# Four groups instead of six through DRAM, fetched one pair earlier, in a mixture of experts

## The chip, the cores and the metric

The kernel runs on one core of one Trainium2 chip. The metric is the device time of one execution in microseconds; the time before is the median of three runs.

## The reference, cut

The program is two blocks of two layers each on 256 tokens of width 1024, in float32. Each layer ends with a hierarchical mixture of experts. What is computed in the first block, where the change is:

```python
def hier_moe(h, wgc, bgc, wgf, bgf, w1, w3, w2):       # 16 experts of width 256, two for each token
    ...                                               # gates: [T, 16], two entries of a row are not zero
    a = jnp.einsum('td,edf->tef', t, w1)
    c = jnp.einsum('td,edf->tef', t, w3)
    act = jax.nn.silu(a) * c * gates[:, :, None].astype(t.dtype)
    y = jnp.einsum('tef,efd->td', act, w2)
    return y.reshape(B, S, D)

# in first_block, for each of its two layers
y_moe = hier_moe(h, ...)
y_ple = jax.nn.sigmoid(h @ ple_wg[i] + ple_bg[i]) * (p[i] @ ple_wp[i])
h = layer_norm(DN_ALPHA * h + y_moe + y_ple, ln2_g[i], ln2_b[i])
```

## The kernel before

The program is written with the Tile framework: the source gives the order of the work, and a scheduler that works at compile time puts every engine's instructions into one fixed queue, in which they run in order; it may move an instruction ahead of earlier ones that it thinks will still wait. `self.behind(r)` (L581) makes what is traced in it stand behind instruction `r` on `r`'s engine.

Weights come from DRAM in tiles of 1 MB, issued by SyncE in the order in which they are used (`w_ahead`, L555). They share 22 slots of 8 KB per partition (`s8`, `NS`) with most of the other large tiles; a new tile waits until the last reader of what was in its slot is done. PSUM's eight banks are two sets of four, `pp` (products that are held) and `ps` (called `pa` in the trace).

`experts` (L1316) is used by both blocks; `far` is true in the first one alone. There each expert has 64 places for tokens, two experts make a group of 128 rows, eight groups are worked on in four pairs (`j` = 0, 2, 4, 6). For a pair:

- `gather` (L1328) brings the tokens of a pair's experts into columns by products with a matrix of zeros and ones (`rD`), one pair ahead.
- `up` (L1346) multiplies by w1 and w3 (32 matmul instructions per group: `pa<-w,xg`). Between the two halves of a pair's second `up` stands `turn` of its first group.
- `turn` (L1358) makes the gated product: SiLU on ScalarE (L1361), a multiplication on VectorE (L1362), two transposes on TensorE (L617), a copy on ScalarE (L1367).
- `down(j, q)` (L1372) multiplies by half `q` of w2 (8 instructions). For the first six groups (`out`) the result goes to a `pp` bank, is copied to SBUF, by ScalarE or VectorE (L1391, L1389), and is written to a table `rows` in DRAM by GpSimd's DMA queue (L1392). For the last two it goes to a `ps` bank and is split into a high and a low part (`split`, L613, L614).
- `fetch` (L1398), at the end of the third pair, brings for each token its at most two rows of the table back by four indirect DMAs on GpSimd's queue (L1403) into two slots `yz`, and adds them to `h` with eight additions on VectorE (L1408). A token without a second row there reads row 0, which is zero. `row_ids` (L1245) works out which rows.
- `combine` (L1413) takes the last two groups back to the tokens by products with the transposed matrix (`rS`, made by `spread`, L1262, with four transposes for a pair of groups, L1271), which add up in four `pp` banks `y`: per group 2 parts x 2 halves x 2 token tiles. `residual` (L644) adds `h` into `y` by products with the identity. The layer norm reads `y`.

The hook `each(j)` runs other work between these steps: in layer 0 the steps of the next layer's filters (on `ps` banks), in layer 1 a piece of the second block's preparation.

In the trace layer 0's mixture lies from about 185 to 315 us, layer 1's from about 500 to 625 us; the last pairs begin at 273.49 and 577.84 us.

Of the kernel before, what the change touches and what calls it, by code (L numbers as in the profile page):

```python
# [12 lines left out]
F32 = mybir.dt.float32  # L13
# [8 lines left out]
D = 1024  # L22
# [8 lines left out]
E1, CAP1 = 16, 64  # L31
E2, CAP2 = 32, 32
NS = 22

AHEAD = {"10": (6, 8, 11, 13, 10), "11": (6, 8, 11, 13, 10), "20": (6, 10, 12, 16, 16), "21": (6, 10, 12, 16, 16)}
WPRI = 20
# [433 lines left out]
class Kern:  # L470
# [303 lines left out]
    def setup(self):  # L774
        nc, I = self.nc, self.I
        self.h = self.s8([128, 2, D], "h")
        self.pc = self.const([128, I["pc"].shape[1]], name="pc")
        for t in range(2):
            nc.sync.dma_start(self.h[:, t, :], I["x"][t * 128:(t + 1) * 128, :])
        nc.sync.dma_start(self.pc, I["pc"])  # L780
        self.ident = self.const([128, 128], name="ident")
        make_identity(nc, self.ident)

        def cut(name, **k):
            o, n = self.L["pc"][name]
            a = self.pc[:, o:o + n]
            return a.rearrange("p (a b) -> p a b", **k) if k else a

        self.rc = cut("rc", a=2)
        self.rs = cut("rs", a=2)  # L790
        self.iota = cut("iota")
        self.key = cut("key")
        self.inv2 = cut("inv2")
        self.identb = self.const([128, 128], BF16, name="identb")
        nc.gpsimd.tensor_copy(self.identb, self.ident)
        self.oneb = self.const([128, 128], BF16, name="oneb")
        nc.gpsimd.memset(self.oneb, 1.0)
        self.ones = self.const([128, 1], name="ones")
        nc.gpsimd.memset(self.ones, 1.0)
        self.identr = self.const([128, 128], F32R, name="identr")  # L800
        nc.gpsimd.tensor_copy(self.identr, self.ident)
        self.selm = self.const([128, 36], name="selm")
        nc.gpsimd.tensor_add(self.selm, self.ident[:, 0:36], self.ident[:, 64:100])

        self.rows = self.dpool.tile([1 + (E1 - 4) * CAP1, D], F32, name="rows")
        zero = self.tmp(D // 128)
        nc.gpsimd.memset(zero, 0.0)
        nc.gpsimd.dma_start(self.rows[0:1, :].rearrange("a (p c) -> (a p) c", p=128), zero)
        self.emask = {}
        for cap in sorted({CAP1, CAP2}):  # L810
            ne = 128 // cap
            m = self.const([128, 2, ne], name=f"em{cap}")
            nc.gpsimd.memset(m, 0.0)
            for i in range(ne):
                nc.gpsimd.memset(m[i * cap:(i + 1) * cap, :, i], 1.0)
            self.emask[cap] = m
# [428 lines left out]
    def row_ids(self, r):  # L1245

        v, cap, E = self.nc.vector, r["cap"], r["E"]
        z = self.tmp(5 * E + 4)
        s, u, base = a2(z[:, 0:2 * E]), a2(z[:, 2 * E:4 * E]), z[:, 4 * E:5 * E]
        v.tensor_scalar(base, self.iota[:, 0:E], float(cap), -float(cap), op0=OP.mult, op1=OP.add)  # L1250
        v.scalar_tensor_tensor(s, r["pos"], float(cap), r["pos"], op0=OP.is_le, op1=OP.mult)
        v.scalar_tensor_tensor(u, s, 0.0, base[:, None, :].to_broadcast([128, 2, E]), op0=OP.is_gt, op1=OP.mult)
        v.tensor_add(s, s, u)
        near = 2 * (128 // cap)
        f = a2(z[:, 5 * E:])
        v.reduce_max(f[:, 0], s[:, :, 0:E - near], axis=AX)
        v.reduce_sum(f[:, 1], s[:, :, 0:E - near], axis=AX)
        v.tensor_sub(f[:, 1], f[:, 1], f[:, 0])
        r["ids"] = a2(r["free"].bitcast(I32))
        v.tensor_copy(r["ids"], f)  # L1260
# [55 lines left out]
    def experts(self, r, th, tl, pre, affine, y=None, each=None, later=(0, 1), begun={}):  # L1316
# [4 lines left out]
        cap, ns = r["cap"], r["ns"]  # L1321
        ne = 128 // cap
        ng = ns // 128
        xgs, pgs, aTs = {}, {}, {}
        gain, shift = affine
        far = y is None

        def gather(b):  # L1328
            if b != 1:
# [28 lines left out]
        def turn(j):  # L1358
            pg = pgs.pop(j)
            a = self.tmp(256)  # L1360
            nc.scalar.activation(a, pg[:, 0:256], AF.Silu, scale=1.0 if r["row"] is None else r["factor"][:, j:j + 1])  # L1361
            v.scalar_tensor_tensor(a, a, r["gate"][:, j:j + 1], pg[:, 256:512], op0=OP.mult, op1=OP.mult)  # L1362
            pt = self.ps()
            for f in range(2):
                self.transp(pt[:, f * 128:(f + 1) * 128], a[:, f * 128:(f + 1) * 128])
            aT = a2(self.tmp(256))
            nc.scalar.activation(aT, a2(pt[:, :256]), AF.Copy)  # L1367
            aTs[j] = aT
# [3 lines left out]
        def down(j, q):  # L1372

            aT = aTs[j]
            c = width(j)
            out = far and j < ng - 2
            py = self.pp() if out else self.ps()
            n, o = q * c // 512, q * c % 512
            for f in range(2):
# [18 lines left out]
        def fetch():  # L1398

            z = [self.s8([128, 2, D], "yz") for _ in range(2)]  # L1400
            for t in range(2):
                for k in range(2):
                    nc.gpsimd.indirect_dma_start(z[k][:, t, :], None, self.rows, bass.IndirectOffsetOnAxis(ap=r["ids"][:, k, t:t + 1], axis=0))  # L1403
            for t in range(2):
                for n in range(2):
                    x = self.h[:, t, n * 512:(n + 1) * 512]
                    for k in range(2):
                        v.tensor_add(x, x, z[k][:, t, n * 512:(n + 1) * 512])  # L1408

        def width(j):  # L1410
            return D // ne if j == ng - 1 else 512

        def combine(j, qs, start=False):  # L1413

            if j not in r["S"]:
                self.spread(r, [j, j + 1])
            c = width(j)
            for z in range(2):
                for q in qs:
# [21 lines left out]
        for j in range(0, ng, 2):  # L1441
# [8 lines left out]
            down(j, 1)  # L1450
            if each:
                each(j + 1)
            if last:
                if far:
                    y = [[self.pp(), self.pp()] for _ in range(2)]
                    combine(j, (0, 1), True)
                    down(j + 1, 0)
                    self.residual(v, y)
                    self.h = self.s8([128, 2, D], "h")
                    down(j + 1, 1)  # L1460
                    combine(j + 1, (0, 1))
                    continue
                self.h = self.s8([128, 2, D], "h")
                combine(j, (0, 1))
                for q in range(D // width(j + 1)):
                    down(j + 1, q)
                    if q:
                        combine(j + 1, (q - 1,))
                combine(j + 1, (q,))
            elif far:  # L1470
                for q in range(2):
                    down(j + 1, q)
                gather(j // 2 + 1)
                if j + 4 == ng:
                    fetch()
                    self.spread(r, [ng - 2, ng - 1])
            else:
                down(j + 1, 0)
                combine(j, (0, 1))
                down(j + 1, 1)  # L1480
                gather(j // 2 + 1)
                combine(j + 1, (0, 1))
# [674 lines left out]
```

## Time and profile before

| | before |
|---|---|
| median of 3 runs | 1358.36 us (1356.62 to 1360.59) |
| profiled execution | 1358.84 us, span 1357.2 us, mean granted TensorE clock 0.951 |
| TensorE busy (matmul) | 1215.0 us, 90% |
| VectorE, ScalarE, GpSimd busy | 647.1, 471.1, 69.6 us |
| read from and written to HBM | 399.94 MB, 7.34 MB |
| GpSimd's DMA queue | 10.49 MB in 3104 packets |

Busy time is a sum over stages with different limits, and a matmul's end is modelled, so 90% doesn't say that TensorE is at its peak. What a stage is worth is read from the timeline of its engines and from what ended each wait. A time in the rows below is in microseconds from the start of the span. PE is TensorE's matmul, PEld its weight load, DVE VectorE, ACT ScalarE, POOL GpSimd, SP SyncE; `x16` counts instructions that the timeline has merged, and an fp32 product counts as two.

### The profile page before, as it was taken

The numbers are of one execution on the slowest core, as the hardware profiler recorded it, in microseconds if no ns is written. First come the engines' busy times: TensorE is split into PE (matmuls) and PEld (weight loads), VectorE is DVE, ScalarE is ACT, GpSimd is POOL, SyncE is SP. The second block draws the span as 40 slices with busy tenths as digits, with TensorE's granted clock in tenths as the row PEclk, the third lists the DMA queues.
The fourth block names the chain that finished last, engine by engine and source line by source line (L and its number), as shares of the span: only waits on it lengthen the run. The fifth ranks groups of instructions, "written<-read, shape, count | busy, mean of one in ns | idle before, by whom it ended". The sixth has DMA issues, their size and how long they took to land. (4 is left out here: it accounts for less than half of the span.)

```text
span 1357.2 us, 17894 instructions
## 1 busy us (share of the span) xinstructions
PE 1215.0 (90%) x6512; PEld 735.0 (54%) x6512; DVE 647.1 (48%) x1840; ACT 471.1 (35%) x971; POOL 69.6 (5%) x95
## 2 busy tenths in 40 slices
PE   6999999979999999958999888787899998978877
PEld 5777754427877763415888432231498676413222
DVE  6867853338778961227776410110487556101011
ACT  4456521215565631205665210110356652100011
POOL 1200000010200000110011000000000101000000
PEclk8899999989999999979999898898999998989989
DMA  9455579996254669998074899999950537999997
GB/s 379 176 206 217 192 276 403 422 414 265 78 218 166 246 238 409 422 414 352 26 280 159 315 413 421 421 422 421 394 238 33 224 118 295 422 421 422 421 421 260
DMA packets 71537, 408.55 MB, mean 301 GB/s; under 512 B 7952, under 2 KB 18448, under 8 KB 26128
## 3 DMA queue, kind: packets, MB, share of 16 engines
q1 hardware_dynamic: 68336, 396.82, 73.0%
q0 software_dynamic: 3104, 10.49, 1.9%
q8 instruction: 54, 0.88, 0.3%
q14 instruction: 43, 0.35, 0.1%
HBM read 399.94 MB, written 7.34 MB: 300 GB/s over the span
## 5 line engine op out<-in xcount | busy, mean ns | idle before, releaser
L604 PE MATMUL pa<-w,xg 128*32 128x512 f32 (+1 forms) x1536 | 304.4, 673 | 52.4 <-DMA w<-in_w 49.5
L604 PEld LDWEIGHTS pa<-w,xg 128*32 128x32 f32 (+1 forms) x1536 | 79.6, 131 | 251.3 <-issue 148.3
L596 DVE TENSOR_TENSOR wlo<-w,whi 128x512 fp32r<-128x512 f32 (+1 forms) x260 | 177.3, 692 | 47.2 <-PE pp L604 37.4
L594 ACT ACTIVATE whi<-w 128x512 fp32r<-128x512 f32 (+1 forms) x260 | 157.9, 628 | 115.8 <-PE pp L604 99.5
L1362 DVE SCALAR_TENSOR_TENSOR tmp<-tmp,rgs,pa 128x256 f32<-128x256 f32 x32 | 15.4, 480 | 308.0 <-ACT tmp L1361 307.8
L604 PE MATMUL pa<-w,tmp 128*32 128x512 f32 (+2 forms) x640 | 122.1, 556 | 10.4 <-DMA w<-in_w 10.2
L614 DVE TENSOR_TENSOR wlo<-pa,whi 128x512 fp32r<-128x512 f32 (+1 forms) x44 | 28.3, 643 | 140.9 <-ACT whi L613 138.5
L604 PE MATMUL pp<-wlo,hTh 128*128 128x512 f32 (+1 forms) x224 | 87.7, 395 | 1.8 <-DVE wlo L596 1.8
L604 PE MATMUL pp<-whi,hTh 128*128 128x512 f32 (+1 forms) x224 | 88.7, 396 | 0.0
L604 PE MATMUL pp<-whi,hTl 128*128 128x512 f32 (+1 forms) x224 | 87.8, 392 | 0.0
L604 PE MATMUL pp<-hTh,wlo 128*128 128x256 f32 x256 | 73.8, 289 | 3.8 <-DVE wlo L596 3.8
L604 PE MATMUL pp<-hTh,whi 128*128 128x256 f32 x256 | 74.3, 291 | 2.5 <-DVE hTh L901 2.5
L604 PE MATMUL pp<-hTl,whi 128*128 128x256 f32 x256 | 73.3, 287 | 0.0
L604 PE MATMUL pa<-rD,th 128*128 128x256 f32 x256 | 67.7, 301 | 1.3 <-DVE row L699 0.8
L604 PEld LDWEIGHTS pa<-w,tmp 128*32 128x32 f32 (+1 forms) x640 | 29.4, 112 | 71.2 <-issue 43.2
L1361 ACT ACTIVATE tmp<-pa,rgs 128x256 f32<-128x256 f32 x16 | 7.6, 473 | 171.5 <-PE pa L604 171.5
L613 ACT ACTIVATE whi<-pa 128x512 fp32r<-128x512 f32 (+1 forms) x44 | 24.6, 558 | 121.2 <-PE pa L604 121.2
L604 PE MATMUL pa<-rD,tl 128*128 128x256 f32 x256 | 65.3, 292 | 0.0
L604 PEld LDWEIGHTS pa<-rD,th 128*128 128x128 f32 x256 | 51.0, 199 | 16.2 <-issue 12.4
L1367 ACT ACTIVATE tmp<-pa 128x256 f32<-128x256 f32 x32 | 12.2, 382 | 127.0 <-PE pa L617 127.0
L604 PEld LDWEIGHTS pp<-hTh,whi 128*128 128x128 f32 x256 | 50.1, 196 | 5.1 <-ACT whi L594 3.4
L604 PEld LDWEIGHTS pp<-hTh,wlo 128*128 128x128 f32 x256 | 50.2, 196 | 4.6 <-DVE wlo L596 4.6
(473 smaller groups left out, 2080.7 us busy)
## 6 DMA issues: line engine op xcount, KB each, us to landing
w<-in_w SPq DMA_DIRECT2D x349, 1024.0 KB, 16.4
w<-in_w SPq DMA_DIRECT2D x32, 256.0 KB, 6.0
gb<-in_row SPq DMA_DIRECT2D x5, 1024.0 KB, 14.2
w<-in_w SPq DMA_DIRECT2D x8, 512.0 KB, 20.5
rows<-whi POOLq DMA_DIRECT2D x12, 256.0 KB, 6.7
rows<-wlo POOLq DMA_DIRECT2D x12, 256.0 KB, 7.1
FI<-in_c SPq DMA_DIRECT2D x4, 512.0 KB, 7.7
w<-in_w SPq DMA_DIRECT2D x2, 640.0 KB
```

The source lines that it names most:

```text
L594: self.nc.scalar.activation(hi, w[:, c0:c0 + c], AF.Copy)
L596: self.nc.vector.tensor_sub(lo, w[:, c0:c0 + c], hi.bitcast(F32))
L604: self.last = self.nc.tensor.matmul(out, lhsT, rhs, start=start, stop=True, skip_group_check=True)
L613: self.nc.scalar.activation(hi, x, AF.Copy)
L614: self.nc.vector.tensor_sub(lo, x, hi.bitcast(F32))
L1361: nc.scalar.activation(a, pg[:, 0:256], AF.Silu, scale=1.0 if r["row"] is None else r["factor"][:, j:j + 1])
L1362: v.scalar_tensor_tensor(a, a, r["gate"][:, j:j + 1], pg[:, 256:512], op0=OP.mult, op1=OP.mult)
L1367: nc.scalar.activation(aT, a2(pt[:, :256]), AF.Copy)
```

## The change

Only groups 0 to 3 go through the DRAM table (`NFAR = 4`). The fetch stands at the end of the second pair, with the spread of groups 4 to 7 behind it. The additions are a function of their own, called in the third pair, and are held behind the VectorE multiplication of group 5's gated product (`turned[nf + 1]`). Groups 4 and 5 are split and combined as the last two are; the four banks `y` are taken in the third pair, and the combine of group 4 starts the sums. The residual's products stand ahead of the last pair's combine. The second block takes the same path as before.

```diff
@@ -31,6 +31,7 @@
 E1, CAP1 = 16, 64
 E2, CAP2 = 32, 32
 NS = 22
+NFAR = 4
 
 AHEAD = {"10": (6, 8, 11, 13, 10), "11": (6, 8, 11, 13, 10), "20": (6, 10, 12, 16, 16), "21": (6, 10, 12, 16, 16)}
 WPRI = 20
@@ -802,7 +803,7 @@
         self.selm = self.const([128, 36], name="selm")
         nc.gpsimd.tensor_add(self.selm, self.ident[:, 0:36], self.ident[:, 64:100])
 
-        self.rows = self.dpool.tile([1 + (E1 - 4) * CAP1, D], F32, name="rows")
+        self.rows = self.dpool.tile([1 + NFAR * 128, D], F32, name="rows")
         zero = self.tmp(D // 128)
         nc.gpsimd.memset(zero, 0.0)
         nc.gpsimd.dma_start(self.rows[0:1, :].rearrange("a (p c) -> (a p) c", p=128), zero)
@@ -1251,10 +1252,10 @@
         v.scalar_tensor_tensor(s, r["pos"], float(cap), r["pos"], op0=OP.is_le, op1=OP.mult)
         v.scalar_tensor_tensor(u, s, 0.0, base[:, None, :].to_broadcast([128, 2, E]), op0=OP.is_gt, op1=OP.mult)
         v.tensor_add(s, s, u)
-        near = 2 * (128 // cap)
+        fe = NFAR * 128 // cap
         f = a2(z[:, 5 * E:])
-        v.reduce_max(f[:, 0], s[:, :, 0:E - near], axis=AX)
-        v.reduce_sum(f[:, 1], s[:, :, 0:E - near], axis=AX)
+        v.reduce_max(f[:, 0], s[:, :, 0:fe], axis=AX)
+        v.reduce_sum(f[:, 1], s[:, :, 0:fe], axis=AX)
         v.tensor_sub(f[:, 1], f[:, 1], f[:, 0])
         r["ids"] = a2(r["free"].bitcast(I32))
         v.tensor_copy(r["ids"], f)
@@ -1321,9 +1322,10 @@
         cap, ns = r["cap"], r["ns"]
         ne = 128 // cap
         ng = ns // 128
-        xgs, pgs, aTs = {}, {}, {}
+        xgs, pgs, aTs, turned = {}, {}, {}, {}
         gain, shift = affine
         far = y is None
+        nf = NFAR if far else 0
 
         def gather(b):
             if b != 1:
@@ -1359,7 +1361,7 @@
             pg = pgs.pop(j)
             a = self.tmp(256)
             nc.scalar.activation(a, pg[:, 0:256], AF.Silu, scale=1.0 if r["row"] is None else r["factor"][:, j:j + 1])
-            v.scalar_tensor_tensor(a, a, r["gate"][:, j:j + 1], pg[:, 256:512], op0=OP.mult, op1=OP.mult)
+            turned[j] = v.scalar_tensor_tensor(a, a, r["gate"][:, j:j + 1], pg[:, 256:512], op0=OP.mult, op1=OP.mult)
             pt = self.ps()
             for f in range(2):
                 self.transp(pt[:, f * 128:(f + 1) * 128], a[:, f * 128:(f + 1) * 128])
@@ -1373,7 +1375,7 @@
 
             aT = aTs[j]
             c = width(j)
-            out = far and j < ng - 2
+            out = j < nf
             py = self.pp() if out else self.ps()
             n, o = q * c // 512, q * c % 512
             for f in range(2):
@@ -1401,19 +1403,22 @@
             for t in range(2):
                 for k in range(2):
                     nc.gpsimd.indirect_dma_start(z[k][:, t, :], None, self.rows, bass.IndirectOffsetOnAxis(ap=r["ids"][:, k, t:t + 1], axis=0))
+            return z
+
+        def add(z):
+
             for t in range(2):
                 for n in range(2):
                     x = self.h[:, t, n * 512:(n + 1) * 512]
                     for k in range(2):
-                        v.tensor_add(x, x, z[k][:, t, n * 512:(n + 1) * 512])
+                        with self.behind(turned[nf + 1]):
+                            v.tensor_add(x, x, z[k][:, t, n * 512:(n + 1) * 512])
 
         def width(j):
             return D // ne if j == ng - 1 else 512
 
         def combine(j, qs, start=False):
 
-            if j not in r["S"]:
-                self.spread(r, [j, j + 1])
             c = width(j)
             for z in range(2):
                 for q in qs:
@@ -1450,16 +1455,16 @@
             down(j, 1)
             if each:
                 each(j + 1)
-            if last:
+            if j < nf:
+                for q in range(2):
+                    down(j + 1, q)
+                gather(j // 2 + 1)
+                if j + 2 == nf:
+                    z = fetch()
+                    self.spread(r, list(range(nf, ng)))
+            elif last:
                 if far:
-                    y = [[self.pp(), self.pp()] for _ in range(2)]
-                    combine(j, (0, 1), True)
-                    down(j + 1, 0)
                     self.residual(v, y)
-                    self.h = self.s8([128, 2, D], "h")
-                    down(j + 1, 1)
-                    combine(j + 1, (0, 1))
-                    continue
                 self.h = self.s8([128, 2, D], "h")
                 combine(j, (0, 1))
                 for q in range(D // width(j + 1)):
@@ -1467,16 +1472,13 @@
                     if q:
                         combine(j + 1, (q - 1,))
                 combine(j + 1, (q,))
-            elif far:
-                for q in range(2):
-                    down(j + 1, q)
-                gather(j // 2 + 1)
-                if j + 4 == ng:
-                    fetch()
-                    self.spread(r, [ng - 2, ng - 1])
             else:
+                start = far and j == nf
+                if start:
+                    add(z)
+                    y = [[self.pp(), self.pp()] for _ in range(2)]
                 down(j + 1, 0)
-                combine(j, (0, 1))
+                combine(j, (0, 1), start)
                 down(j + 1, 1)
                 gather(j // 2 + 1)
                 combine(j + 1, (0, 1))
```

## Rows read from the trace of the kernel before

**Rows 1.** Page, section 2: DMA busy tenths, 40 slices of 33.9 us.

```profile
DMA  9455579996254669998074899999950537999997
```

**Rows 2.** TensorE timeline, layer 0, last pair: start, us, line, tiles, count, wait.

```profile
273.49 10.52 PE L604 MATMUL pa<-w,xg 128*64 128x512 f32 x48
293.29 0.69 PE L617 MATMUL pa<-ident,tmp 128*128 128x128 f32 x2 [9.28 <-DVE tmp L1362]
293.91 5.04 PE L604 MATMUL pa<-w,xg 128*64 128x512 f32 x16
...
302.84 0.73 PE L604 MATMUL pp<-whi,rS 128*128 128x512 f32 x2
303.40 0.63 PE L604 MATMUL pp<-wlo,rS 128*128 128x512 f32 x2
...
313.57 0.63 PE L604 MATMUL pp<-whi,rS 128*128 128x512 f32 x2
314.03 0.86 PE L604 MATMUL pp<-wlo,rS 128*128 128x512 f32 x3
```

**Rows 3.** VectorE timeline, layer 0, last pair; in brackets idle time and releaser.

```profile
284.87 1.29 DVE L1408 TENSOR_TENSOR h<-h,yz 128x512 f32<-128x512 f32 x2 [9.84 <-DMA yz<-rows,rgs]
...
290.89 1.29 DVE L1408 TENSOR_TENSOR h<-h,yz 128x512 f32<-128x512 f32 x2 [0.26 <-DMA yz<-rows,rgs]
...
292.76 0.47 DVE L1362 SCALAR_TENSOR_TENSOR tmp<-tmp,rgs,pa 128x256 f32<-128x256 f32 x1
```

**Rows 4.** TensorE timeline, layer 1, last pair.

```profile
577.46 0.45 PE L1271 MATMUL pa<-identr,rD 128*128 128x128 f32 x4
577.84 10.52 PE L604 MATMUL pa<-w,xg 128*64 128x512 f32 x48
603.08 0.69 PE L617 MATMUL pa<-ident,tmp 128*128 128x128 f32 x2 [14.72 <-DVE tmp L1362]
603.70 5.45 PE L604 MATMUL pa<-w,xg 128*64 128x512 f32 x16
...
624.25 0.86 PE L604 MATMUL pp<-wlo,rS 128*128 128x512 f32 x3
```

**Rows 5.** VectorE timeline, layer 1, last pair.

```profile
601.34 1.29 DVE L1408 TENSOR_TENSOR h<-h,yz 128x512 f32<-128x512 f32 x2 [0.65 <-DMA yz<-rows,rgs]
602.55 0.47 DVE L1362 SCALAR_TENSOR_TENSOR tmp<-tmp,rgs,pa 128x256 f32<-128x256 f32 x1
```

**Rows 6.** Stage table: stretch, length, busy PE, PEld, DVE, ACT, POOL; granted clock, DMA share, GB/s.

```profile
600.00:605.00 5.00, 1.92 (x6) 0.82 (x8) 2.37 (x5) 0.38 (x1) 0.00 (x0) 0.50 1.07 405
```

**Rows 7.** TensorE timeline, third pair of layers 0 and 1.

```profile
261.94 1.98 PE L604 MATMUL pa<-fz,fz 64*128 64x512 f32 x4
...
567.85 0.44 PE L617 MATMUL pa<-ident,tmp 128*128 128x128 f32 x2
568.22 5.37 PE L604 MATMUL pp<-w,tmp 128*64 128x512 f32 x24
```

**Rows 8.** GpSimd timeline, the first fetch of each layer.

```profile
277.44 1.03 POOL L1403 DMA_INDIRECT yz<-rows,rgs  x1 [8.36 <-PE pa L604]
...
583.04 1.01 POOL L1403 DMA_INDIRECT yz<-rows,rgs  x1 [7.84 <-issue]
```

**Rows 9.** Row writes: page, section 6 (issue to landing last); then the GpSimd timeline.

```profile
rows<-wlo POOLq DMA_DIRECT2D x12, 256.0 KB, 7.1
...
241.04 0.54 POOL L1392 DMA_DIRECT2D rows<-wlo  x1 [1.27 <-DVE wlo L1389]
...
548.83 0.54 POOL L1392 DMA_DIRECT2D rows<-wlo  x1 [1.30 <-DMA w<-in_w]
...
574.65 0.54 POOL L1392 DMA_DIRECT2D rows<-wlo  x1 [1.30 <-DVE wlo L1389]
```

**Rows 10.** Weight DMAs of the window 567 to 575 us: issues, time to landing.

```profile
L567 SPq DMA_DIRECT2D w<-in_w x3: 327/327/328, 568.2 to 573.6; - x3
...
DMA to landing us min/median/max: 24.8/25.2/25.6
```

## The prediction

> **What bounds the kernel now.** I read four views, in this order. First the utilisation rows of the page. The row of DMA shares shows what carries a saving to the end: shortly after each of the first block's two mixtures of experts the DMA engines fall to between 0 and 5 tenths, and again between the two later mixtures [rows 1]. So nothing that the first block gains is given back by the weight stream further on. Stages in which DMA idles are paced by compute, and what is late there moves everything behind it. (The page's chain of waits reaches back only into the last mixture, where weights set the pace, and says nothing of the first block.)
>
> Then the TensorE timeline of the last expert pair, in both layers. In layer 0 the up products run without a gap from 273.49 for 10.52 us, to 284.0; then TensorE stands for 9.28 us until the two transposes of group 6's gated product [rows 2]. In layer 1 the same place costs 14.72 us, from 588.4 to 603.1 [rows 4]. TensorE waits for the gate multiplication on VectorE (L1362).
>
> Third, VectorE's timeline shows why that multiplication is late: its queue runs in order, and the eight adds of the fetched rows (L1408) stand ahead of it. They wait for the indirect DMAs: 9.84 us for the first in layer 0, and the last pair starts at 290.89; in layer 1 the last pair starts at 601.34. The multiplication follows at 292.76 and 602.55 [rows 3, 5]. Fourth, the stage table: around 600 us TensorE is hardly busy, DMA is at 1.07 of its share, and the granted clock is 0.50, the lower level, 1.2 GHz [rows 6]. The second half of group 7's up product therefore takes 5.04 us in layer 0 and 5.45 us in layer 1 [rows 2, 4]. At full clock 48 such instructions take 10.52 us, so 16 take 3.5 us.
>
> **The change part by part.**
>
> *Removed: the stand in the last pair.* Fetch and adds move one pair ahead, so the multiplication of group 6 no longer has an add ahead of it. Layer 0: 9.28 us of waiting, 5.04 - 3.5 = 1.54 us of half-speed products, and the two transposes at 0.69 us [rows 2] instead of 0.44 us [rows 7], together 11.1 us. Layer 1: 14.72 + 1.95 + 0.25 = 16.9 us. Gross 28.0 us, all on TensorE's path.
>
> *Added: sixteen accumulating products per layer.* Groups 4 and 5 now go through the combine: per group 2 parts x 2 halves x 2 token tiles = 8 products of 128x512. In the tail of layer 0 two of them start 0.56 us ahead of the next ones (302.84 to 303.40), and another two 0.46 us (313.57 to 314.03) [rows 2]; so 0.23 to 0.28 us each. I take 0.26, between the two. 16 x 0.26 = 4.2 us per layer. No cover: TensorE is busy throughout that pair.
>
> *Added: four more transposes* to spread four groups instead of two. The four of layer 1 hold TensorE for 577.84 - 577.46 = 0.38 us [rows 4]; another 0.4 us. They stand at the end of pair 2 now, so pair 3 starts 0.8 us later.
>
> *Evictions.* Each layer loses four copies and four writes to DRAM of 256 KB, and gains four splits of two instructions each, so four more instructions on ScalarE and VectorE together. They lie beside TensorE's down and gather products, and the last pair already works in just this way, with its combine products closely spaced [rows 2]. I cost them at nothing; without that cover each of the four down products would hold TensorE for a low part, some 0.65 us (estimate: half of a pair of adds [rows 3]), 5 us in both layers. The eight adds are the same ones, at another place. On POOL's queue the four issues of the fetch, about 1 us each [rows 8], stand where pair 3's four row writes stood; SP's queue keeps its order, and the fetch brings the same bytes a pair earlier.
>
> *Residual and y.* The residual's products move ahead of the last combine; their number is the same. y takes its four PSUM banks from pair 3 on. No price.
>
> *The moved wait: the adds behind group 5's gate product.* Queued behind them on VectorE are the low parts of groups 4 and 5, which the combines need, and the evictions of the last gather. What counts is when the rows land. The last write of pair 2 is issued at 241.04 (layer 0) and 548.83 (layer 1), and lands 7.1 us later by the median of twelve; the fetch follows such a landing by 583.04 - 574.65 - 7.1 = 1.3 us [rows 8, 9]. So the fetch starts at 249.4 and 557.2. From its first issue to the last add pair it took 290.89 - 277.4 = 13.5 us in layer 0 and 601.34 - 583.0 = 18.3 us in layer 1 [rows 3, 5, 8]. With 1.29 us for the last two adds and 0.7 us for one low part, the first combine has all it needs at 264.9 and 577.5.
>
> TensorE needs it when combine 4 is through its four high-part products. Layer 1: group 5's transposes at 567.85, then two blocks of eight down products of the 24 that take 5.37 us (1.8 us each) [rows 7], 0.8 us of shift and 1.0 us of high parts: 568.2 + 3.6 + 0.8 + 1.0 = 573.6 (568.2 is where the down products begin). So TensorE waits 577.5 - 573.6 = 3.9 us. Layer 0: the filter's products start at 261.94 and take 1.98 us [rows 7], then one block of eight: 263.9 + 1.8 + 0.8 + 1.0 = 267.5, after 264.9: no wait. Bounds: nothing at all if layer 1's rows land as fast as layer 0's did (557.2 + 13.5 + 2.0 = 572.7), and no gain beyond that; upwards, see the second rival. I take 3.9 us, since the load on DMA in layer 1's pair 3 is that of its own pair 4.
>
> The Trainium skill, "DMA: Bandwidth & Descriptors", section "Anatomy of one DMA — SWDGE (gpsimd) path", gives about 2.0 us plus bytes over 436 GB/s per transfer, and in "Queues, rings and completion order" says that an engine takes turns between its queues. By that, 4 x 512 KB in turns with the weights would land in some 10 us (estimate from that page), there would be no wait in layer 1, and the sum would be the first rival's. The traces disagree with it: 13.5 and 18.3 us were measured.
>
> *Weights.* The next thing that could be late is the weight stream. The last down weights of group 6 in layer 1 are issued at 573.6 and land 25.6 us later, at 599.2 [rows 10]. The change takes 1 MB of writes out of the way, about 2.5 us at the 405 GB/s of [rows 6], so 596.7; the fetch is still ahead of it either way. TensorE gets there at 577.84 + 0.4 + 4.2 + 3.9 + 10.52 + 0.4 + 3.5 = 600.8. So weights are just not the bound; if they were, TensorE would wait for each us beyond 4.1.
>
> *The sum.* 28.0 - 2 x (4.2 + 0.4) - 3.9 = 14.9 us. The profiled execution's 1358.84 us (1.6 us more than its span, 0.5 us above the median of the runs) becomes 1343.9, so **1344 us**.
>
> **The rivals.**
>
> *1. The rows land before the adds are reached.* For: layer 0's fetch was fast. Against: layer 1's was not. Then 28.0 - 9.2 = 18.8 us: 1340.
>
> *2. The fetch is held back, and the stand only moves into pair 3: slower.* The two fetch buffers (L1400) come out of the same 22 slots as the weights, and must wait until TensorE has read what was in them. If the slots are ones that pair 3 itself reads, the fetch starts d us late. TensorE then waits d - 2.6 us in layer 0 and d + 3.9 us in layer 1, 2d + 1.3 together; this eats the 18.8 us from d = 8.8 us on. With slots read last by group 4's down products (near 260 and 568 [rows 7], d about 11) it is 23.3 us of waiting and 1363 us. For: in layer 0 POOL's wait ended with TensorE's up products. Against: it ended at 277.44, less than 4 us into them [rows 2, 8]. A moderate d of 4 gives 9.3 us of waiting, and 1349.
>
> *3. The weight stream ends last.* Buffers for rows and for four spread groups hold three slots during pair 3; if the stream falls three tiles of 1 MB behind (7.5 us at the same rate), group 6's weights land at 604.2, TensorE waits 3.4 us more: 1347. For: little room in layer 1. Against: DMA is saturated there with 25 us between issue and landing, so fewer transfers in flight need not idle it.
>
> *4. It does not do what it says*: other waiting work takes the place of the adds ahead of the gate product, and TensorE stands as long as before. Then nothing is gained and the 9.2 us of products are added: 1368. Nothing in [rows 3, 5] but the adds stands there waiting.
>
> **How the numbers follow.** Forecast 0.50 (1344), rival 1 0.12 (1340), rival 3 0.09 (1347), rival 2 with a small d 0.12 (1349), with d between 6 and 10 0.08 (1354 to 1361), with more 0.06 (1363), rival 4 0.03 (1368). A measurement of this kernel can tell about 0.3%, 4 us, from no change: 1354.3 to 1362.4. Faster are the first four, 0.83, of which 0.03 is taken off for a small d that is not so small; same is 0.08 with these 0.03 and 0.01 of the rest, 0.12; slower 0.08. For 8 in 10 the range takes in rival 1 with combine products at 0.23 us (1 us less), and some 4 us of waits in the last pair that go with it, 1335, and rival 2 with a small d, 0.28 us per product and the weights' wait on top, 1355.
>
> **What would show it.** No gap of TensorE after group 7's first half in the last pair, and granted clock 1.00 there; sixteen more accumulating products per layer in pair 3; the adds on VectorE behind group 5's gate product, the last of them near 265 and 577 us; in layer 1 a gap of about 4 us on TensorE before or in combine 4, none in layer 0; the last combine products of the two mixtures, now at 314.03 and 624.25 [rows 2, 4], 6.5 and 14.9 us earlier, and everything after shifted by the latter. Wrong it would be if the fetch is issued later than 2 us after its rows have landed, if TensorE waits for weights at group 6's down product, or if the shift is lost in the stages behind.

## The result and the profile after

The changed kernel takes 1339.68 us (median of 4, 1338.71 to 1340.6) beside 1359.24 us for the kernel before: a ratio of 0.9858, 95% interval [0.9841, 0.9876]. Two later sets of runs of it gave 0.9855 [0.9833, 0.9877] and 0.9852 [0.9828, 0.9877]. The forecast was 1344 us in a range of 1335 to 1355, faster. The profiled execution took 1339.96 us, with a span of 1338.3 us, 18.9 us less than before; 14.9 us were forecast.

The page of the changed kernel (share of the span; tenths in 40 slices; queue rows):

```profile
PE 1215.0 (91%) x6552; PEld 737.9 (55%) x6552; DVE 650.2 (49%) x1844; ACT 475.5 (36%) x977; POOL 64.9 (5%) x87
...
DMA  9455569997254669999166799999942537999997
...
q0 software_dynamic: 2464, 8.39, 1.6%
...
HBM read 399.94 MB, written 5.25 MB: 303 GB/s over the span
```

TensorE has the busy time that it had, though it does 32 more combine products: before, some of its products ran at half speed. DMA still has the idle slices behind both mixtures that [rows 1] showed, and what follows layer 1 takes 731.7 us beside 732.1, so nothing was given back there. GpSimd's queue (`q0`) and the writes have lost 2.1 MB.

TensorE's timeline of the last pairs, layer 0 and then layer 1 (start, us, instruction, count, wait in brackets), against [rows 2, 4]:

```profile
278.71 10.52 PE L605 MATMUL pa<-w,xg 128*64 128x512 f32 x48
289.16 0.44 PE L618 MATMUL pa<-ident,tmp 128*128 128x128 f32 x2
289.52 3.65 PE L605 MATMUL pa<-w,xg 128*64 128x512 f32 x16
...
307.68 0.63 PE L605 MATMUL pp<-wlo,rS 128*128 128x512 f32 x2
...
577.01 10.52 PE L605 MATMUL pa<-w,xg 128*64 128x512 f32 x48
587.46 0.44 PE L618 MATMUL pa<-ident,tmp 128*128 128x128 f32 x2
587.83 3.65 PE L605 MATMUL pa<-w,xg 128*64 128x512 f32 x16
```

No bracket stands in them. The waits of 9.28 and 14.72 us are gone, the transposes take 0.44 us, and the second half 3.65 us instead of 5.04 and 5.45. The stage table of the stretch shows the upper clock level where [rows 6] had 0.50:

```profile
577.00:588.00 11.00, 11.00 (x53) 3.73 (x54) 0.48 (x1) 0.45 (x2) 0.00 (x0) 1.00 1.01 418
```

VectorE in layer 0's third pair, where the adds (L1415) now are, then two rows of layer 1's; against [rows 3, 5]:

```profile
259.15 0.48 DVE L1364 SCALAR_TENSOR_TENSOR tmp<-tmp,rgs,pa 128x256 f32<-128x256 f32 x1 [6.97 <-ACT tmp L1363]
259.55 1.28 DVE L1415 TENSOR_TENSOR h<-h,yz 128x512 f32<-128x512 f32 x2
262.90 0.69 DVE L1415 TENSOR_TENSOR h<-h,yz 128x512 f32<-128x512 f32 x1 [2.06 <-DMA yz<-rows,rgs]
263.51 0.68 DVE L615 TENSOR_TENSOR wlo<-pa,whi 128x512 fp32r<-128x512 f32 x1
264.11 0.68 DVE L1415 TENSOR_TENSOR h<-h,yz 128x512 f32<-128x512 f32 x1
266.60 0.69 DVE L1415 TENSOR_TENSOR h<-h,yz 128x512 f32<-128x512 f32 x1 [1.81 <-DMA yz<-rows,rgs]
267.21 0.68 DVE L615 TENSOR_TENSOR wlo<-pa,whi 128x512 fp32r<-128x512 f32 x1
...
270.38 2.02 DVE L1415 TENSOR_TENSOR h<-h,yz 128x512 f32<-128x512 f32 x3 [0.90 <-DMA yz<-rows,rgs]
...
567.51 0.68 DVE L615 TENSOR_TENSOR wlo<-pa,whi 128x512 fp32r<-128x512 f32 x1
570.85 1.29 DVE L1415 TENSOR_TENSOR h<-h,yz 128x512 f32<-128x512 f32 x2 [2.65 <-DMA yz<-rows,rgs]
```

The adds still wait for the indirect DMAs, but the gate product (L1364) is ahead of them, and the low parts that the combines need (L615) stand between them. The fetch starts 0.8 and 1.1 us after its last row has landed, at 248.67 and 550.28 on GpSimd:

```profile
248.67 1.03 POOL L1405 DMA_INDIRECT yz<-rows,rgs  x1 [7.32 <-DMA rows<-wlo]
...
550.28 1.01 POOL L1405 DMA_INDIRECT yz<-rows,rgs  x1 [6.13 <-PE pa L605]
```

Its last rows land 21.7 us (270.35) and 20.5 us (570.76) after that first issue; before, this took 13.4 and 18.2 us.

All that it costs TensorE in layer 1 as a gap is this, in the combine of group 4:

```profile
565.75 1.20 PE L605 MATMUL pp<-whi,rS 128*128 128x512 f32 x4
566.79 0.62 PE L605 MATMUL pp<-wlo,rS 128*128 128x512 f32 x2
568.25 0.74 PE L605 MATMUL pp<-wlo,rS 128*128 128x512 f32 x2 [0.84 <-DVE wlo L615]
```

In layer 0 a low part holds up a product of the last gather instead:

```profile
273.05 0.39 PE L605 MATMUL pa<-rD,th 128*128 128x256 f32 x1 [0.41 <-DVE wlo L615]
```

In the two repeats of the changed kernel layer 0 has no such gap, and layer 1 has 1.12 and 0.17 us in one and 0.66 us in the other.

The pairs of all kernels, in us of TensorE's timeline from the first up product of one pair to that of the next, the last pair to the end of its last combine product:

| kernel (what is different) | layer 0: pairs 2, 3, 4 | layer 1: pairs 2, 3, 4 | median us |
|---|---|---|---|
| before | 29.1, 29.9, 41.4 | 25.8, 26.1, 47.3 | 1359.24 |
| changed | 29.9, 34.6, 29.6 | 26.5, 31.3, 29.6 | 1339.68 |
| changed, again (a_again) | 29.9, 33.6, 29.6 | 26.5, 31.9, 29.6 | 1339.58 |
| changed, again (a_third) | 29.9, 33.6, 29.6 | 26.5, 31.3, 29.6 | 1337.28 |
| a_unheld (adds not held) | 29.9, 45.8, 29.6 | 26.5, 46.2, 29.6 | 1366.43 |
| a_solid (adds in one block) | 29.9, 38.4, 29.6 | 26.5, 38.6, 29.6 | 1352.61 |
| b_nofetch (before, no fetch) | 29.1, 29.9, 30.4 | 25.8, 26.1, 33.4 | 1335.26 |
| a_nofetch (changed, no fetch) | 29.9, 33.6, 29.6 | 26.5, 29.9, 29.6 | 1335.80 |
| n2 (two groups through DRAM) | 34.0, 33.6, 29.6 | 33.1, 29.9, 29.6 | 1348.66 |
| n6_gate (six, adds held) | 29.1, 29.9, 30.4 | 25.8, 26.1, 40.1 | 1339.17 |
| n6_low (six, adds held further back) | 29.1, 29.9, 35.8 | 25.8, 26.1, 44.3 | 1342.84 |
| n64 (six, then four) | 29.1, 29.9, 30.4 | 26.5, 31.6, 29.6 | 1334.95 |
| a_small (weights in 2 KB runs) | 27.9, 42.8, 31.2 | 26.5, 36.4, 33.3 | 1355.31 |
| a_solid_small (both) | 27.9, 41.5, 30.7 | 26.5, 38.2, 32.0 | 1353.18 |

The first pair of layer 0 (29 to 35 us) and what follows layer 1 (730 to 736 us) vary from one execution to the next by as much, in kernels that leave them alone; so pairs 2 to 4 are compared, and of the medians those of runs on the same chip.

### The profile page after: what moved, and what is told of

Read it like the earlier page. It is cut to its first block, busy times and chain, and to the rows that moved or that the text cites. A ratio compares the mean times of both kernels' runs of the same rounds, so it can differ in the third digit from the quotient of the medians.

```text
span 1338.3 us, 17964 instructions
## 1 busy us (share of the span) xinstructions
PE 1215.0 (91%) x6552; PEld 737.9 (55%) x6552; DVE 650.2 (49%) x1844; ACT 475.5 (36%) x977; POOL 64.9 (5%) x87
## 5 line engine op out<-in xcount | busy, mean ns | idle before, releaser
L605 PE MATMUL pa<-w,xg 128*32 128x512 f32 (+1 forms) x1536 | 295.2, 648 | 53.8 <-DMA w<-in_w 50.6
L1364 DVE SCALAR_TENSOR_TENSOR tmp<-tmp,rgs,pa 128x256 f32<-128x256 f32 x32 | 15.4, 480 | 318.3 <-ACT tmp L1363 318.0
L605 PE MATMUL pa<-w,tmp 128*32 128x512 f32 (+2 forms) x704 | 139.8, 560 | 11.6 <-DMA w<-in_w 11.3
L615 DVE TENSOR_TENSOR wlo<-pa,whi 128x512 fp32r<-128x512 f32 (+1 forms) x52 | 33.7, 649 | 135.6 <-ACT whi L614 133.4
L605 PEld LDWEIGHTS pa<-w,tmp 128*32 128x32 f32 (+1 forms) x704 | 33.3, 114 | 83.3 <-issue 51.4
L614 ACT ACTIVATE whi<-pa 128x512 fp32r<-128x512 f32 (+1 forms) x52 | 29.2, 564 | 129.4 <-PE pa L605 126.3
L605 PEld LDWEIGHTS pa<-rD,tl 128*128 128x128 f32 x256 | 51.6, 201 | 1.7 <-issue 1.6
## 6 DMA issues: line engine op xcount, KB each, us to landing
w<-in_w SPq DMA_DIRECT2D x8, 512.0 KB, 16.9
```

The source lines that it names most:

```text
L605: self.last = self.nc.tensor.matmul(out, lhsT, rhs, start=start, stop=True, skip_group_check=True)
L614: self.nc.scalar.activation(hi, x, AF.Copy)
L615: self.nc.vector.tensor_sub(lo, x, hi.bitcast(F32))
L1364: turned[j] = v.scalar_tensor_tensor(a, a, r["gate"][:, j:j + 1], pg[:, 256:512], op0=OP.mult, op1=OP.mult)
```

## Experiments

**1. The hold taken away, and the adds put in one block.** Which property of the new place makes the gain: that it is a pair earlier, or the order on VectorE's queue? In a_unheld the adds are free to be queued ahead of the gate products, and the scheduler puts all eight ahead of both, group 4's too:

```diff
-                        with self.behind(turned[nf + 1]):
+                        if True:
```

> The changed kernel with the eight additions not held behind group 5's gate product; nothing else is edited. Theory (VectorE's order decides: what matters is whether a gate product is queued behind additions that wait for the fetch): the additions then stand ahead of group 4's gate product (VectorE, 251.7 and 553.3 us in the changed kernel's trace), while the last rows land at 270.4 and 570.8; TensorE, which is through the first half of group 5's up product at 254.6 and 556.1, stands until about 272 and 573: some 17 us in each layer, and 2 us each at the lower clock after it, less the 0.8 us that it waits now. About 1376 us, slower than the kernel before. Rival (the gain comes from the earlier fetch and from fewer writes, and the hold is worth little): within 2 us of 1340.

It took 1366.43 us, a ratio of 1.0068 [1.0046, 1.009]: slower than before. VectorE of a_unheld in layer 0:

```profile
255.77 0.69 DVE L1415 TENSOR_TENSOR h<-h,yz 128x512 f32<-128x512 f32 x1 [13.34 <-DMA yz<-rows,rgs]
```

and TensorE of it, layers 0 and 1:

```profile
263.51 0.69 PE L618 MATMUL pa<-ident,tmp 128*128 128x128 f32 x2 [10.60 <-DVE tmp L1364]
...
580.25 0.69 PE L618 MATMUL pa<-ident,tmp 128*128 128x128 f32 x2 [14.31 <-DVE tmp L1364]
```

The old stands are back, one pair earlier, and the added products are paid as well. Fetching earlier alone gains nothing. The stands are shorter than the 17 us expected, and the time is 10 us under the 1376 expected, since the rows landed 13.2 and 18.5 us after the first issue, not 21.7 and 20.5.

In a_solid the gate product stays ahead, but all eight adds stand in one block ahead of the low part of group 4's second half, close to what the prediction had supposed:

```diff
-            self.split(py[:, :c], yh[:, :c], yl[:, :c])
+            nc.scalar.activation(yh[:, :c], py[:, :c], AF.Copy)
+            with self.behind(low.pop("after", None)):
+                v.tensor_sub(yl[:, :c], py[:, :c], yh[:, :c].bitcast(F32))
...
-                            v.tensor_add(x, x, z[k][:, t, n * 512:(n + 1) * 512])
+                            low["after"] = v.tensor_add(x, x, z[k][:, t, n * 512:(n + 1) * 512])
```

> The changed kernel with all eight additions held ahead of the low part of group 4's second half (the scheduler had put that low part between the fifth and the sixth addition). Theory A (the forecast's wait of 3.9 us in layer 1 was not paid because the low parts run between additions): the combine of group 4 then waits for the last rows, which land at 270.4 and 570.8 us, plus two additions and the low part: to about 273 and 574, where it now goes on at 267.3 and 568.3; 5 to 6 us in each layer, about 1350 us. Theory B (the combine is not held by these additions at all, something else covers): 1340.

1352.61 us, 0.9957 [0.9939, 0.9975], and these gaps on TensorE:

```profile
266.38 0.74 PE L605 MATMUL pp<-wlo,rS 128*128 128x512 f32 x2 [2.98 <-DVE wlo L1399]
...
572.51 1.22 PE L605 MATMUL pp<-wlo,rS 128*128 128x512 f32 x2 [4.67 <-DVE wlo L1399]
```

The third pairs grow to 38.4 and 38.6 us, 3.8 to 4.8 and 6.7 to 7.3 us over the changed kernel's. That is more than the gaps, for behind them products run at the lower clock (the granted clock is 0.87 in the mean of 263 to 276 us and 0.80 of 566 to 583). So the wait that the prediction priced exists when the adds form a block, in both layers; the scheduler's interleaving is what keeps it off TensorE.

**2. Both kernels without fetch and adds** (`fetch()` and `add(z)` deleted, so the first groups' rows are missing from the sum). This prices the fetch and its adds by themselves in each kernel.

> The kernel before without fetch and additions: the rows of six groups are written to DRAM, but not fetched or added (this part of the sum is left out). Theory: the standing of TensorE in the last pair and the lower clock behind it are all that goes: 11.8 us in layer 0 and 17.7 us in layer 1, by the changed kernel's last pairs (29.43 us each against 41.24 and 47.11), 1329.7 us. Rival (the transfers of the fetch also slow the weights or products beside them): below 1326.

> The changed kernel without fetch and additions (this part of the sum is left out). If the forecast's wait of 3.9 us in layer 1 is there, hidden somewhere in the third pair: 1335.8 us. If only the 0.84 us that the trace shows ahead of the low part's products is paid: 1338.8 us. Its distance from the kernel before without fetch and additions is the price of the added products and transposes, forecast 9.2 us.

1335.26 us, 0.9835 [0.9811, 0.9859], and 1335.80 us, 0.9838 [0.9812, 0.9865]. Without the fetch the times of the two kernels are not told apart. Their distance, forecast 9.2 us, is 0.5; in the traces pairs 2 to 4 are 4.4 us longer in the changed one (179.1 against 174.7), which intervals of some 3.5 us to either side don't resolve. 1335.80 is the number expected if a wait of 3.9 us were hidden in layer 1, but its interval takes in the other number, 1338.8, as well; the traces have to decide. The changed one without it has third pairs of 33.6 and 29.9 us: beside 34.6 and 31.3 that leaves 1.0 and 1.4 us for fetch and adds (in the two repeats 0.0, and 1.4 to 2.0). Beside the third pairs of before it is 3.7 and 3.8 us longer. The kernel before without it does not reach 1329.7 us, for in layer 1 the last pair takes 33.4 us, not 30.4 as in layer 0. TensorE there:

```profile
576.69 3.22 PE L604 MATMUL pa<-w,xg 128*64 128x512 f32 x13 [0.33 <-DMA w<-in_w]
...
581.73 1.93 PE L604 MATMUL pa<-w,tmp 128*64 128x512 f32 x6 [1.39 <-DMA w<-in_w]
```

Behind the stand in layer 1 the weight stream is the next bound. There the added products are mostly free, for TensorE would have stood for weights anyway: pairs 2 to 4 take 85.3 us without them and 86.0 with them, against 89.4 and 93.1 in layer 0.

**3. Only two groups through DRAM.** Do fewer row writes help, or is each group that is combined just a price?

```diff
-NFAR = 4
+NFAR = 2
```

> The changed kernel with two groups through DRAM instead of four (NFAR = 2): fetch at the end of the first pair, additions in the second. Against the changed kernel 16 more accumulating products and four more transposes in each layer, and 2.1 MB less written. By the third pairs of the two kernels without fetch (33.6 against 29.9 us and 29.9 against 26.1 us) the products take 3.75 us a layer: with 0.4 us of transposes 8 us more than the changed kernel, 1348 us. Rival (the fewer writes are a part of the gain, 2.5 us per MB at the measured rate): about 1335 us.

1348.66 us, 0.9922 [0.9898, 0.9945]. That is the price of the added products that was expected, with no sign that fewer writes give anything back. The wait behind the adds is in it too: it has gone from layer 1's third pair, which takes 29.9 us as without a fetch, to the second:

```profile
548.67 0.73 PE L605 MATMUL pp<-wlo,rS 128*128 128x512 f32 x2 [2.72 <-DVE wlo L615]
```

**4. The hold without the move.** n6_gate keeps six groups and the old place of the fetch, and holds the adds behind group 7's gate product; n6_low holds them behind the low part of group 7's first half.

```diff
-NFAR = 4
+NFAR = 6
...
+                start = far and j == nf
+                if start:
+                    add(z)
+                    y = [[self.pp(), self.pp()] for _ in range(2)]
+                    combine(j, (0, 1), True)
+                    down(j + 1, 0)
+                    self.residual(v, y)
+                    self.h = self.s8([128, 2, D], "h")
+                    down(j + 1, 1)
+                    combine(j + 1, (0, 1))
+                    continue
```

> Six groups through DRAM and the fetch at the end of the third pair as before, but with the additions held behind group 7's gate product; in the last pair combine 6, down 7, residual, combine 7. No product is added against the kernel before. Theory A (all that was wrong with the kernel before was the queue on VectorE): the stands of 9.3 and 14.7 us and the lower clock behind them go, no products are added: about 1332 us, better than the changed kernel. Theory B (the weights are the next bound in layer 1, and a fetch beside a running TensorE takes 20 us and more from its first issue to its last landing, as in the changed kernel: 21.7 and 20.5): in layer 0 the rows land near 299 and the residual waits, in layer 1 group 6's down product waits for weights until about 21 us after the pair's begin: some 9 us gained in either layer, about 1340 us, no better than the changed kernel.

> As the kernel with six groups and the additions behind group 7's gate product, but with the additions held behind the low part of group 7's first half. Theory A: 1332 us, no different. Theory B: combine 6 no longer waits for rows, the residual does instead, and the weights' wait in layer 1 stays: 1337 to 1341 us.

n6_gate took 1339.17 us, 0.9859 [0.9837, 0.9881], the time of the changed kernel; n6_low 1342.84 us, 0.9898 [0.9867, 0.993]. The time of n6_gate is the rival's (theory B), but its reason only half: in layer 0 the last pair takes 30.4 us, as without any fetch, and the rows are there by 289.66, not 299. Layer 1 loses the gain again, to weights. TensorE of n6_gate:

```profile
580.49 3.65 PE L605 MATMUL pa<-w,xg 128*64 128x512 f32 x14 [2.97 <-DMA w<-in_w]
...
588.00 2.97 PE L605 MATMUL pa<-w,tmp 128*64 128x512 f32 x6 [2.62 <-DMA w<-in_w]
```

n6_low came out 2 us above the 1337 to 1341 us of its theory B, with an interval that overlaps n6_gate's; holding the adds further back gained nothing. Its pairs in the table are not comparable as they stand: some 4.5 of the 5.4 us that its last pair in layer 0 is longer, and 2.0 of the 4.2 us in layer 1, are products of other work (`pa<-fz,FI`, `pa<-WB,kr`) that in n6_gate run behind the pair.

So the hold is enough in layer 0, and the move earns its price in layer 1 alone: pairs 2 to 4 take 87.4 us with it and 92.0 without.

**5. Six groups in layer 0, four in layer 1.** The two best layers together, beside the changed kernel on the same chip.

```diff
-NFAR = 4
+NFAR = (6, 4)
...
-        nf = NFAR if far else 0
+        nf = r["nf"] = NFAR[int(pre[-1])] if far else 0
```

> Six groups through DRAM in layer 0, with the adds behind group 7's gate product in the last pair; four groups in layer 1, as in the changed kernel. If the trace of the six-group version carries over, layer 0's second, third and last pairs take 29.1 + 29.9 + 30.4 = 89.4 us instead of the changed kernel's 29.9 + 34.6 + 29.6 = 94.1, and layer 1 stays at 26.5 + 31.3 + 29.6: about 1335 us, ratio about 0.983. The rival: the weight stream or a wait behind layer 0 takes the gain back (the stages between the two mixtures lengthen beyond 181.6 us, or layer 1's last pair again waits for weights): about 1339.5 us, ratio 0.986, the same as the changed kernel.

> The changed kernel, unedited, beside the version with six and four groups on the same chip: 1339.6 us, ratio 0.986.

1334.95 us, 0.9828 [0.9805, 0.9852], against 1337.28 us, 0.9852 [0.9828, 0.9877]. In the traces layer 0's pairs 2 to 4 take 89.4 us instead of 93.1, and the stages between the mixtures stay at 181.6 us. TensorE's last pair of layer 0:

```profile
270.15 10.52 PE L605 MATMUL pa<-w,xg 128*64 128x512 f32 x48
280.60 0.44 PE L618 MATMUL pa<-ident,tmp 128*128 128x128 f32 x2
280.97 3.65 PE L605 MATMUL pa<-w,xg 128*64 128x512 f32 x16
```

It is faster than before, and its 2.3 us beside the changed kernel agree with the trace in sign; by the times alone the two aren't told apart, their intervals overlap.

The repeat of the changed kernel that ran beside experiments 3 and 4 gave 1339.58 us:

> The changed kernel itself on the chip of these runs, to compare with: 1340 us, in the third pairs TensorE's gap of 0.8 us in layer 1 and none in layer 0.

**6. What sets the fetch's pace.** The rows landed some 13 us after the first issue in some stretches and 18 to 22 us in others. One difference in the queue rows (packets, MB, share of 16 engines) is the size of the weights' packets. The changed kernel's third pair, layer 0, 259 to 270 us:

```profile
q1 hardware_dynamic: 452, 3.31, 71.8%
q0 software_dynamic: 379, 1.36, 30.4%
```

n6_gate's last pair, layer 0, 283 to 290 us:

```profile
q0 software_dynamic: 401, 1.44, 52.3%
q1 hardware_dynamic: 681, 1.36, 51.7%
```

The fetch's packets are 3.6 KB in the mean in both. The weights' (`q1`) are 7.3 KB in the first, where the fetch gets 30%, and 2.0 KB in the second, where it gets 52%: there the last group's weights come in runs of 512 numbers. (Both are the later part of a fetch; in the earlier, while its four transfers are being issued, it has 19.4 and 23.7%.) The kernel before shows the same between its two layers: 56.0% against 1.9 KB in layer 0 from 283 to 291 us, 39.5% against a mean of 3.2 KB in layer 1 from 592 to 601. That could be queues that take turns by the packet. To test it, the weights of ten experts per layer were brought in by 2 KB runs, in the changed kernel and in a_solid:

```diff
-                self.nc.sync.dma_start(t[:, :c], self.I["w"][o][:, :c])
+                k = 512 if n[:3] in ("x10", "x11") and n[3:].rstrip("d") in SMALL else c
+                for b in range(0, c, k):
+                    self.nc.sync.dma_start(t[:, b:b + k], self.I["w"][o][:, b:b + k])
```

> The changed kernel, but the weights of experts 4 to 13 of the first block are brought in by four transfers of 512 columns for each tile instead of one of 2048, so in runs of 2 KB instead of 8 KB; bytes and order are the same. The traces so far: with weight packets of 7.3 KB in the mean the fetch has some 30% of the DMA engines in the third pairs and its last rows land 20.5 to 21.7 us after its first issue; with weight packets of 1.9 KB, in the last pair of layer 0, it has 52 to 56% and takes 13.4 us. Theory (the queues take turns by the packet, so the share follows from the sizes): the fetch's share in the third pairs rises to some 50%, the last rows land some 14 us after the first issue, and the small waits of layer 1's third pair vanish: 1338 us, ratio 0.985, unless the weights, which are now the slower ones, come late. Rival (the fetch's pace hangs on something else in the last pair, say how full the weight slots are): share near 30%, 20 to 22 us, 1339.6 us.

> The same edit on the version with all eight adds ahead of the low part, where the landing of the rows is seen in the time: that version measured 1352.6 us, with gaps of 2.98 and 4.67 us on TensorE and third pairs of 38.4 and 38.6 us. Theory (turns by the packet): the rows land some 6 us sooner, both gaps vanish, the third pairs go back to 33.6 and about 31 us, and the time to about 1341 us. Rival (the pace hangs on something else): the gaps stay, 1352 us.

The pace moved as the theory has it, the time did not: 1355.31 us, 0.9981 [0.9966, 0.9996], and 1353.18 us, 0.9968 [0.9951, 0.9985]. The queue rows of a_small's third pair, layer 0, 246 to 253 us:

```profile
q0 software_dynamic: 446, 1.62, 58.9%
q1 hardware_dynamic: 611, 1.12, 44.2%
```

The last of the four indirect DMAs of layer 1 (count, us from issue to landing) in the changed kernel,

```profile
yz<-rows,rgs POOLq DMA_INDIRECT x1, 16.6
```

in a_small,

```profile
yz<-rows,rgs POOLq DMA_INDIRECT x1, 9.6
```

and TensorE of a_small in layer 0's third pair:

```profile
255.76 4.91 PE L608 MATMUL pa<-w,xg 128*64 128x512 f32 x13 [2.92 <-DMA w<-in_w]
```

With 1.8 KB weight packets the fetch has 59% and its last rows land 13.0 and 13.4 us after the first issue; a_solid_small shows no gap behind a low part any more. But what the fetch won, the weights lost: weight loads now wait for DMA in the third pairs, which take 42.8 and 36.4 us. How much of that is the fetch's larger share and how much the slower small runs (364 GB/s in 255 to 270 us, after the fetch, where the kernel before moved 423 GB/s in 249 to 262 us) was not separated. Nor was the size of the runs from the number of transfers, four where there was one.

## Why the prediction was right, and where it was off

**The forecast and its sign were right, by the mechanism it named.** The stand was VectorE's queue, with adds that wait for DMA ahead of a product that TensorE needs; a_unheld puts them back and the stand with them. The fetch was not held back by its buffers (rival 2: it was issued 0.8 and 1.1 us after its rows had landed, within the 2 us named), no weight was late in the last pairs (rival 3), and no other work took the adds' place (rival 4). The last combine products end 6.6 us earlier in layer 0 (forecast 6.5) and 18.5 us earlier in layer 1 (forecast 14.9).

The terms, in us, from the table of pairs; 30.4 us is a last pair with neither a stand nor the moved residual (b_nofetch and n6_gate, layer 0):

| term | forecast | measured |
|---|---|---|
| stand of layer 0 | 11.1 | 41.4 - 30.4 = 11.0 |
| stand of layer 1 | 16.9 | 47.3 - 30.4 = 16.9 |
| residual moved ahead of the last combine | 0 | 2 x (30.4 - 29.6) = 1.6 |
| added products and transposes | -9.2 | -(0.8 + 3.7 + 0.7 + 3.8) = -9.0 |
| evictions | 0 | nothing left in the line above |
| wait of the combines for low parts | -3.9 | -(1.0 + 1.4) = -2.4 |
| sum | 14.9 | 18.1 |

In layer 1 the 16.9 us come from stand and move together: n6_gate, which takes away the stand alone, wins 47.3 - 40.1 = 7.2 there and leaves the rest to the weights.

The other 0.8 of the 18.9 us lies outside pairs 2 to 4, and is within what these stretches vary by.

**The stand** was sized to a tenth of a microsecond, by its gap, the half-speed products behind it and the slow transposes. Reading the clock of the stretch was worth the effort: the gaps alone are 24.0 of these 27.9 us.

**Residual: "no price" was wrong**, in the gain's favour. With it at the old place the last pair waits 0.34 us for its split, as in n64's trace, and takes 0.8 us more. It was not tried alone: the 0.8 us is what is left between last pairs that do the same work in another order, and the part that isn't this wait has no cause shown.

```profile
294.91 1.02 PE L605 MATMUL pp<-whi,identr 128*128 128x512 f32 x2 [0.34 <-ACT whi L652]
```

**The wait behind the adds: two steps failed, and they largely cancelled, which was luck.** First, the time "From its first issue to the last add pair", 13.5 us in layer 0 and 18.3 us in layer 1, was carried over from the last pair to the third as a length. But the length changed with the packets that the fetch shared the engines with. In the third pair the weights come in runs of 8 KB, and the fetch took 21.7 and 20.5 us, 8.2 and 2.2 more. Second, "queued behind them on VectorE are the low parts": all eight adds were taken as one block ahead of every low part. The trace shows low parts after the third, the fifth and the last adds. With the late rows and a block, TensorE would have waited in both layers, as a_solid shows; with the late rows and the interleaving its gaps were 0.41 us in layer 0 and 0.84 us in layer 1, and the third pairs were 2.4 us longer in all. The term that the forecast put at 3.9 us in layer 1 alone was thus 1.0 and 1.4 us, and rival 1's 1340 us came true without its premise: the rows did not land before the adds were reached, they landed later than forecast.

The Trainium skill, "DMA: Bandwidth & Descriptors", section "Queues, rings and completion order", says that each DMA engine takes turns between its queues at packet granularity. The prediction's 10 us for 4 x 512 KB is what equal halves would give. With the sizes put in, equal turns would give the fetch a third of the engines' time for 3.6 KB against 7.3 KB (30.4% measured), 64% against 2.0 KB (52.3% measured) and two thirds against 1.8 KB (58.9% measured). So the rows agree in the direction, and the fetch always got less. It also got fewer packets: 379 to the weights' 452, 401 to 681 and 446 to 611, where strict turns between two queues that both always have work would give as many to either. Whether the fetch had a packet ready at every turn no run shows, so the mechanism stays open.

**Weights: "just not the bound" held**, and more narrowly than it reads: without the added products (b_nofetch) or with the fetch in the last pair (n6_gate) layer 1 does stand for weights. That taking writes out of the way helps the stream, as the prediction has it, no run shows: n2 takes out more and shows no gain from it.

**What the prediction did not ask** is whether the move was needed. It treated move and hold as one edit. The hold alone gives the same total (1339.17 us).

## What to carry to other kernels

An instruction that waits for a DMA can hold up what is queued behind it on its engine, as the adds on VectorE did here (13.34 us in a_unheld, and TensorE with them for 10.60): look first for a product that a busier engine needs behind it, and put that ahead of the waiting instruction before moving any transfer. Before a transfer's time is carried from one stretch to another, compare the packet sizes of what it will share the DMA engines with: here the same fetch took 13.4 us in one and 21.7 us in the other. Price move and order separately, layer by layer: here the order was free and the move cost 4.5 us a layer, which was paid back only in the layer that the weights bound next.

## What the runs showed of the hardware

The indirect fetch of four transfers took between 13.0 and 21.7 us beside the weight stream, and its pace went with the size of the other queue's packets: in its later part 30% of the engines' time against 7.3 KB packets, 52% against 2.0 KB, 59% against 1.8 KB. Alone it had 70.5% in the mean of 256 to 260 us in a_unheld, where TensorE stood and the weight queue was all but empty; the stretch takes in the fetch's end, where its share runs out, so this is no upper bound:

```profile
q0 software_dynamic: 294, 1.04, 70.5%
q1 hardware_dynamic: 2, 0.01, 0.5%
```

Beside large weight packets the fetch took less from the weight stream; making them small sped the fetch up by 7 to 9 us, and the kernel lost some 16 us (1355.31 against 1339.58), of which, as said, the part of the smaller runs alone is not known.
